# Two feed-forward layers that take over the buffers of the mixing stage before them

## The chip, the cores and the metric

The kernel runs as one launch on one core of a Trainium2 chip. A core has five engines that work from their own instruction queues: TensorE (PE, matrix products and transposes), VectorE (DVE), ScalarE (ACT), GpSimd (POOL) and SyncE (SP, which here issues nearly all transfers), and 16 DMA engines. The metric is the device time of one execution in microseconds (us). The kernel before takes 2841.91 us, the median of 3 runs that lie between 2841.21 and 2844.3 us.

## What is computed

Two transformer blocks, one behind the other, on a sequence of 1024 rows of 1024 float32 values. Each block mixes the rows (several kinds of attention, a convolution, a pooling), brings the mixed values back with a matrix `w_out`, and then runs a feed-forward network of 2816 channels. Cut to what surrounds the change:

```python
# first block
mix = concatenate([att, conv, pool], axis=-1)          # 1024 x 1024
x = x + mix @ w_out
h2 = rms_norm(x, norm2_g)
up = causal_depthwise_conv(h2 @ w_up, ffn_dw_w)        # 2 x 2816 columns
gate, val = split(up, 2)
x = x + (silu(gate) * val) @ w_down

# second block
merged = g_a * (y_a @ w_branch_a) + g_b * (y_b @ w_branch_b)
x = x + rmsnorm(merged @ w_out, post_mix_w)
h = rmsnorm(x, pre_ffn_w)
f = (silu(h @ w_gate) * (h @ w_up)) @ w_down
x = x + rmsnorm(f, post_ffn_w)
```

## The kernel before

**Numbers as pairs.** Every matrix operand is split into a rounded high part (a cast on ACT) and the rest (raw minus high, by DVE or POOL), and each product is three matmuls, high x high, low x high, high x low. A wide matmul has 512 columns. The tiles of a pair end in `h` and `l` (`T1h`, `T1l`), or are both called `w`.

**Stages, in the order of time.** `mix1` (attention, convolution, pooling) to about 420 us; `out1`, the first out projection, to 519.66; the first feed-forward layer's way up (`ffn_up`) to about 985 and its way down (`ffn_down`) to about 1200; `mix2` to about 1950 and `merge2` to about 2048; `out2`, the second out projection, to 2145; the second way up to 2610, the way down to the end. The program is written as a sequence of calls; a list scheduler puts each engine's instructions into one fixed order when the kernel is built, and on the chip each engine works that order off and waits on semaphores.

**The way up.** The 1024 rows and the inner dimension are halved, and per channel group of 128 seven products replace eight (a Strassen-like scheme). The seven right-hand operands `T1` to `T7` are normed rows, or sums of row blocks (L765 to L768 in `pre_row`), transposed through PE into a PSUM tile `tr` (L744) and split into high (ACT, L747) and low (DVE, L748) by `put`. `T1` and `T2` need rows 0 to 3 alone and are put as those rows come out of the out projection; the other five need rows 4 to 7, and their twenty puts follow the opening of the way up's own pools in the order `LATE = (6, 5, 7, 4, 3)`. The left-hand operands are 128 columns of the weights and sums of their quarters, split by ACT (L800) and, in turn, by POOL and DVE (`lo_of`, L787). A product goes into PSUM tiles `x`, `y` or `z`, which ACT copies (L843 snap).

**Pools.** `mixing` (L106) holds three pools for a mix and its out projection: `hT` (transposed rows, high and low, two halves), `w` (weights) and `ps` (PSUM, all eight banks). They close when the out projection is done; then `ffn` opens `fw` (weights), `fT` (T3 to T7) and a PSUM pool `fps`. A tile of a new pool can be written when the last readers and writers of the space below it are done.

**out1** (L690): row i takes two halves of 24 matmuls into `mm`, DVE adds each to the row in place (L706), then `done` stores the row to DRAM (`x1D`, L755), norms it in place (L186 to L188: square on ACT, mean and root on POOL, product on DVE) and puts it. **out2** (L1297) computes halves of eight rows (`first`, `second`) with half the weights each; per row two squares on ACT (L1318), POOL's sum and root, two products on DVE (L1323), the add (L1325), the store to `x3D` (L1326) and the norm. Rows come back from DRAM by eight loads on SP's queue (L1302), and its last three weight loads stand behind them.

The lines of a weight pair, which the prediction follows on ACT and POOL:

```python
# before, ffn_up
def split(raw, w):
    hi, lo = (fw.tile([P, 1024], F32R, tag="w", ...)[:, :w] for _ in range(2))
    nc.scalar.copy(out=hi, in_=raw)      # L800
    self.lo_of(lo, raw, hi)              # L787: POOL and DVE in turn
```

Of the kernel before, what the change touches and what calls it, by code (L numbers as in the profile page):

```python
# [41 lines left out]
LATE = (6, 5, 7, 4, 3)  # L42
# [39 lines left out]
class Net:  # L82
# [607 lines left out]
    def out1(self, rows, pp, done):  # L690
# [27 lines left out]
        gB, jk = (self.wpool.tile([P, D], F32, tag="wr", name=self.n("wr"), bufs=2) for _ in range(2))  # L718
        nc.sync.dma_start(out=gB, in_=I["norm2_g"][0].partition_broadcast(P))
# [13 lines left out]
    def early_T(self, name):  # L733

        keep, sums = ExitStack(), ExitStack()
        pool = keep.enter_context(self.pool(name, 1, side="right"))
        T = {i: tuple(pool.tile([P, 4, 512], F32R, tag=f"T{i}{x}", name=self.n(f"T{i}{x}")) for x in "hl") for i in (1, 2)}
        return keep, sums, sums.enter_context(self.pool(name + "s", 3, side="right")), T
# [11 lines left out]
    def pre_row(self, i, rows, keep, gB, jk, T, pool, ps):  # L750
# [3 lines left out]
        if keep is not None:  # L754
            nc.sync.dma_start(out=keep[i * P:(i + 1) * P, :], in_=x)  # L755
        self.norm_rows(x, x, jk, gB)
# [12 lines left out]
        self.sums[j] = {6: t2, 5: b11, 7: k0, 4: b21, 3: k1}  # L769

    def ffn(self, R, T, close_sums, close_T, Wg, cg, Wu, cu, Wd, conv, keep, done):

        gD = self.dram.tile([NF // 2, 7, P, 512], F32, tag=f"gD{int(conv)}", name=self.n("gD"))
        with self.pool("fw") as fw, self.pool("fT") as fT, self.pool("fps", 2, PSUM) as ps:
            self.ffn_up(T, fT, fw, R, ps, Wg, cg, Wu, cu, conv, gD, close_sums)
# [13 lines left out]
    def ffn_up(self, T, fT, fw, R, ps, Wg, cg, Wu, cu, conv, gD, close_sums):  # L789
        nc = self.nc  # L790
        chans, raws, pts = {}, {}, {}
# [4 lines left out]
        snaps = {1: t1, 2: t2, 3: t3}  # L796

        def split(raw, w):
            hi, lo = (fw.tile([P, 1024], F32R, tag="w", name=self.n("w"), bufs=8)[:, :w] for _ in range(2))
            nc.scalar.copy(out=hi, in_=raw)  # L800
            self.lo_of(lo, raw, hi)
            return [(hi[:, o:o + 512], lo[:, o:o + 512]) for o in range(0, w, 512)]

        def weights_a(c, queue=nc.sync):

            r = [fw.tile([P, 2, 512], F32, tag="wr", name=self.n("wr"), bufs=3) for _ in range(2)]
            for t, W, col in ((r[0], Wg, cg + c * P), (r[1], Wu, cu + c * P)):
                queue.dma_start(out=t.rearrange("p h (k m) -> p (h k) m", k=4),
                                in_=W[:, col:col + P].rearrange("(k p) m -> p k m", p=P))
            A = chans[c] = {}  # L810
            A[1], A[2] = split(r[0].rearrange("p h x -> p (h x)"), 1024)
            raws[c] = r

        def weights_b(c):

            r = raws.pop(c)
            A = chans[c]
            a11, a12, a21, a22 = r[0][:, 0], r[0][:, 1], r[1][:, 0], r[1][:, 1]
            u, v = (fw.tile([P, 2, 512], F32, tag="ws", name=self.n("ws"), bufs=2) for _ in range(2))
            nc.vector.tensor_tensor(out=u[:, 0], in0=a21, in1=a22, op=ALU.add)  # L820
            nc.vector.tensor_tensor(out=u[:, 1], in0=u[:, 0], in1=a11, op=ALU.subtract)
            A[5], A[6] = split(u.rearrange("p h x -> p (h x)"), 1024)
            nc.vector.tensor_tensor(out=v[:, 0], in0=a11, in1=a21, op=ALU.subtract)
            nc.vector.tensor_tensor(out=v[:, 1], in0=a12, in1=u[:, 1], op=ALU.subtract)
            A[7], A[3] = split(v.rearrange("p h x -> p (h x)"), 1024)
            A[4], = split(a22, 512)

# [11 lines left out]
        def begin(c):  # L839
            pts[c] = {n: ps.tile([P, 512], F32, tag=n, name=self.n(n)) for n in ("y", "x", "z")}  # L840

        def snap(c, j):
            nc.scalar.copy(out=snaps[j], in_=pts[c]["x"])  # L843
# [20 lines left out]
        def p3(c):  # L864
            product(c, 3, "y", False)
            add(c, G[:, 514:], "y", t2)
# [29 lines left out]
        for c in (0, 1):  # L896
            weights_a(c, nc.scalar)
        for i in (3, 4, 6, 7, 5):
            T[i] = tuple(fT.tile([P, 4, 512], F32R, tag=f"T{i}{x}", name=self.n(f"T{i}{x}")) for x in "hl")
# [546 lines left out]
```

## Time and profile before

| | |
|---|---|
| median of 3 runs (lowest, highest) | 2841.91 us (2841.21, 2844.3) |
| profiled execution, its own time | 2845.55 us |
| its span, first to last instruction | 2843.8 us |
| mean granted clock of TensorE over the span | 0.980 |
| PE busy | 2687.9 us (95%), 13686 matmuls |
| DVE busy | 1798.9 us (63%) |
| ACT busy | 1200.4 us (42%) |
| POOL busy | 891.6 us (31%) |

The busy share of PE is a mean over stages in which it never stops and stages in which it waits. Two things make PE late: idle time, and stretches in which its granted clock is at the lower of its two levels (1.2 instead of 2.4 GHz), where a matmul takes up to twice as long though PE counts as busy. So a stretch is read by three numbers together: busy time, number of matmuls, granted clock.

### The profile page before, as it was taken

The page shows a single profiled execution, that of the slowest core. Times are in us where ns is not written, and L with a number is a line of the kernel's source. Part 1 is how long each engine was busy: PE and PEld are TensorE (multiplying, and loading weights), DVE is VectorE, ACT ScalarE, POOL GpSimd, SP SyncE. Part 2 cuts the span into 40 slices and gives each one's busy share as a digit, 9 for nine tenths or more (in the row PEclk, how much of TensorE's full clock was granted, in tenths as well). Part 3 has the DMA queues.
Part 4 walks back from the last instruction along what each step waited for, and adds up shares of the span by engine and source line. Part 5 has one row for each costly group of instructions (what it writes and reads, how often), then busy time and mean ns, then how long its engine had stood idle before and what let it go on. Part 6 is the DMA issues. An engine that isn't in the chain of part 4 may idle for free.

```text
span 2843.8 us, 37039 instructions
## 1 busy us (share of the span) xinstructions
PE 2687.9 (95%) x13686; PEld 2258.3 (79%) x13686; DVE 1798.9 (63%) x2748; ACT 1200.4 (42%) x1879; POOL 891.6 (31%) x626
## 2 busy tenths in 40 slices
PE   8999889899999999999999999998997999999997
PEld 7799767678888778788888978887776788887786
DVE  4697574668878799736766443443427555555977
ACT  4344562344544543425545344444323333334333
POOL 3256322123333134611112254422423111211345
PEclk9999999999999999999999999999998999999999
DMA  5445342223332563265554495415412233335722
GB/s 182 122 124 146 115 158 97 82 78 100 107 111 97 207 244 122 93 194 139 155 162 128 126 209 140 133 62 180 157 77 78 82 102 106 111 101 191 260 89 93
DMA packets 317678, 374.01 MB, mean 132 GB/s; under 512 B 42613, under 2 KB 215089, under 8 KB 316985
## 3 DMA queue, kind: packets, MB, share of 16 engines
q1 hardware_dynamic: 309176, 367.45, 41.9%
q10 hardware_dynamic: 8320, 4.19, 0.5%
q8 instruction: 108, 1.77, 0.3%
q14 instruction: 74, 0.60, 0.1%
HBM read 256.49 MB, written 115.08 MB: 131 GB/s over the span
## 4 chain that ended last, share of the span: by engine, by line
PE 69%; DVE 10%; DMA 10%; issue 4%; POOL 3%; ACT 2%; SPq 1%; DVEq 0%; POOLq 0%; ACTq 0%
PE x L118 21%; PE mm L118 20%; PE y L118 11%; PE sc L118 5%; PE z L118 4%; PE pv L118 4%; DVE ac L550 2%; PE tr L359 2%; DVE x L1000 1%; DMA x<-in_w_down_dram 1%; PE tr L1105 1%; DMA x<-gD 1%; DMA mixD<-pvt 1%; DMA wr<-in_w_out_dram 1%; DVE r L1010 1%
## 5 line engine op out<-in xcount | busy, mean ns | idle before, releaser
L139 POOL TENSOR_TENSOR wl<-wr,wh 128x1024 fp32r<-128x1024 f32 x71 | 179.8, 2536 | 359.2 <-ACT wh L138 300.6
L787 POOL TENSOR_TENSOR hl<-x,hl 128x1024 fp32r<-128x1024 f32 x63 | 172.3, 2750 | 278.7 <-ACT hl L1031 197.9
L1031 ACT CAST hl<-x 128x1024 fp32r<-128x1024 f32 x154 | 153.2, 1050 | 221.9 <-PE x L118 123.5
L317 ACT ACTIVATE t<-t,mx 128x640 f32<-128x640 f32 (+3 forms) x192 | 172.9, 901 | 164.6 <-DVE mx L313 156.9
L118 PE MATMUL x<-hl,hl 128*128 128x512 f32 x704 | 214.1, 391 | 3.6 <-DVE hl L787 3.6
L787 POOL TENSOR_TENSOR w<-ws,w 128x1024 fp32r<-128x1024 f32 x44 | 135.4, 3078 | 250.7 <-ACT w L800 250.7
L787 POOL TENSOR_TENSOR w<-wr,w 128x1024 fp32r<-128x1024 f32 (+1 forms) x44 | 85.7, 1947 | 397.7 <-ACT w L800 397.7
L118 PE MATMUL mm<-hA,wh 128*128 128x512 f32 x608 | 197.6, 399 | 4.7 <-ACT gs L1231 4.7
L118 PE MATMUL mm<-hB,wh 128*128 128x512 f32 x608 | 196.7, 397 | 1.0 <-ACT gs L1231 1.0
L365 DVE TENSOR_TENSOR pl<-tr,ph 128x512 fp32r<-128x512 f32 (+2 forms) x160 | 100.5, 634 | 120.0 <-DMA yD<-pvt 42.6
L334 POOL TENSOR_SCALAR t<-t,rs 128x640 f32<-128x640 f32 (+7 forms) x128 | 107.4, 846 | 201.9 <-DVE rs L333 159.8
L877 DVE SCALAR_TENSOR_TENSOR r<-r,fdw,r 128x1024 f32<-128x1024 f32 x88 | 122.2, 1406 | 72.2 <-ACT r L875 72.1
L118 PE MATMUL y<-hl,hl 128*128 128x512 f32 x528 | 161.0, 390 | 5.7 <-DVE hl L787 5.7
L118 PE MATMUL mm<-wh,hB 128*128 128x256 f32 (+1 forms) x752 | 162.2, 305 | 3.0 <-ACT hB L180 3.0
L800 ACT CAST w<-wr 128x1024 fp32r<-128x1024 f32 (+1 forms) x88 | 73.6, 838 | 216.2 <-PE x L118 126.0
L118 PEld LDWEIGHTS x<-hl,hl 128*128 128x128 f32 x704 | 132.8, 189 | 32.3 <-DVE hl L787 4.8
L118 PE MATMUL mm<-wh,hA 128*128 128x256 f32 (+1 forms) x704 | 150.6, 301 | 6.3 <-ACT hA L180 2.1
L787 DVE TENSOR_TENSOR hl<-x,hl 128x1024 fp32r<-128x1024 f32 x91 | 140.7, 1553 | 8.7 <-ACT hl L1031 8.4
L118 PE MATMUL x<-hl 128*128 128x512 f32 x352 | 134.2, 393 | 4.9 <-DVE r L1010 4.7
L118 PEld LDWEIGHTS mm<-hA,wh 128*128 128x128 f32 x608 | 115.5, 192 | 29.2 <-ACT gs L1231 5.3
L843 ACT COPY r<-x 128x512 f32<-128x512 f32 x132 | 76.7, 581 | 145.4 <-PE x L118 87.1
L364 ACT CAST ph<-tr 128x512 fp32r<-128x512 f32 (+2 forms) x160 | 85.2, 542 | 123.7 <-PE tr L359 85.9
(350 smaller groups left out, 7720.5 us busy)
## 6 DMA issues: line engine op xcount, KB each, us to landing
gD<-r SPq DMA_DIRECT2D x154, 256.0 KB
x<-gD SPq DMA_DIRECT2D x154, 256.0 KB
wr<-in_w_up_dram SPq DMA_DIRECT2D x60, 512.0 KB
wr<-in_w_in_dram SPq DMA_DIRECT2D x50, 512.0 KB
x<-in_w_down_dram SPq DMA_DIRECT2D x88, 256.0 KB
wr<-in_w_gate_dram SPq DMA_DIRECT2D x20, 512.0 KB
wr<-in_w_out_dram SPq DMA_DIRECT2D x16, 512.0 KB
QS<-q2D SPq DMA_DIRECT2D x32, 256.0 KB
```

Source lines behind the costliest of these rows:

```text
L118: self.nc.tensor.matmul(out, lhsT, rhs, start=start, stop=stop, **kw)
L139: g = (lo_engine or nc.gpsimd).tensor_tensor(out=lo, in0=raw[:, :n], in1=hi.bitcast(F32), op=ALU.subtract)
L317: nc.scalar.activation(out=t[:, :nb * P], in_=t[:, :nb * P], func=AF.Exp, scale=-1.0, bias=m, accum_out=s)
L334: nc.gpsimd.tensor_scalar(out=t[:, :nb * P], in0=t[:, :nb * P], scalar1=r, scalar2=1.0, op0=ALU.mult, op1=ALU.mult)
L359: nc.tensor.transpose(tr[:, o * P:(o + 1) * P], ts[qb][:, c:c + P], self.ident)
L364: nc.scalar.copy(out=ph[:, :w], in_=tr[:, :w])
L365: nc.vector.tensor_tensor(out=pl[:, :w], in0=tr[:, :w], in1=ph[:, :w].bitcast(F32), op=ALU.subtract)
L787: return eng.tensor_tensor(out=lo, in0=raw, in1=hi.bitcast(F32), op=ALU.subtract)
L800: nc.scalar.copy(out=hi, in_=raw)
L843: nc.scalar.copy(out=snaps[j], in_=pts[c]["x"])
L877: nc.vector.scalar_tensor_tensor(out=t, in0=src[:, 2 - s:2 - s + S], scalar=self.fdw[:, 2 - s, cc:cc + 1], in1=t, op0=ALU.mult, op1=ALU.add)
L1031: nc.scalar.copy(out=hi, in_=raw)
```

## The change

The number of matmuls stays the same. The pools `hT` and `ps` of the mix now stay open through the way up, and close behind it (`close_mixing`). The way up's PSUM tiles take the mix's tags (`y` in `sc`, `x` in `mm`, `z` in `pv` or `sc`). T6 and T5 lie in the first halves of `hT` (`hA0`, `hB0`), T7 and T4 in the second, and only T3 in the pool `fT`. The puts of T6 and T5 move into the loop over rows 4 to 7, so 12 puts stay late. The first weight tile of the way up is loaded during the out projection and split there, by ACT and DVE (`w_early`), and the first pairs of channels 0 and 1 behind it are split by DVE instead of POOL. `out1` adds into a tile `o` (two buffers) and stores and norms from there. `out2` takes rows in turn: four halves first, then per row both halves, into one tile `o` (one buffer), with four of its eight weight pairs loaded by `pair_in` and split by DVE; the row loads stand ahead of `merge2`'s last weights in SP's queue.

```diff
-LATE = (6, 5, 7, 4, 3)
+LATE = (7, 4, 3)
...
-        with self.pool("hT", 2) as self.hpool, self.pool("w", 3) as self.wpool, self.pool("ps", 2, PSUM) as self.ps_mix:
+        stack = ExitStack()
+        self.hpool = stack.enter_context(self.pool("hT", 1))
+        self.ps_mix = stack.enter_context(self.pool("ps", 2, PSUM))
+        self.close_mixing = stack.close
+        with self.pool("w", 3) as self.wpool:
             yield
...
+    def T_in(self, t, h):
+        tile_ = self.h_tile(t, h)
+        return tile_[:, :4, :], tile_[:, 4:, :]
...
# out1
-        for i in range(NB):
-            part(i, 0, w0)
-            part(i, 1, w1[6:] if i < 4 else w1)
-            done(i, gB, jk)
+        with self.pool("pe") as pe:
+            gB = self.bcast_row(I["norm2_g"][0], pe)
+            self.w_early(pe.tile([P, D], F32, tag="o", name=self.n("o"), bufs=2))
+            for i in range(NB):
+                o = pe.tile([P, D], F32, tag="o", name=self.n("o"), bufs=2)
+                part(i, 0, w0, o)
+                part(i, 1, w1[6:] if i < 4 else w1, o)
+                done(i, gB, o)
...
# pre_row
+        if i == 4:
+            T[6], T[5] = self.T_in("hA", 0), self.T_in("hB", 0)
...
-        self.sums[j] = {6: t2, 5: b11, 7: k0, 4: b21, 3: k1}
+        self.put(T, 6, j, t2, ps)
+        self.put(T, 5, j, b11, ps)
+        self.sums[j] = {7: k0, 4: b21, 3: k1}
...
+    def w_early(self, raw):
+        raw = self.w_load(0, 0, raw.rearrange("p (h x) -> p h x", h=2))
+        self.w_split(0, (1, 2), raw.rearrange("p h x -> p (h x)"), self.nc.vector)
...
# ffn_up
-            pts[c] = {n: ps.tile([P, 512], F32, tag=n, name=self.n(n)) for n in ("y", "x", "z")}
+            pts[c] = {n: ps.tile([P, 512], F32, tag=t, name=self.n(n), bufs=b)
+                      for n, t, b in (("y", "sc", 3), ("x", "mm", 2), ("z", *(("sc", 3) if c % 2 else ("pv", 1))))}
...
         for c in (0, 1):
-            weights_a(c, nc.scalar)
+            weights_a(c, nc.vector)
...
# merge2
-            ws += self.pair(W, 6, 1, pool=po, th="wph", tl="wpl", bufs=1)
+            ws += self.pair_in(W, 6, 1, pp.tile([P, S], F32, tag="g0", name=self.n("g")), [(self.wpool, "wr", 2)] * 2)
...
+    def pair_in(self, W, k, dh, raw, hl):
+        nc = self.nc
+        nc.sync.dma_start(out=raw.rearrange("p (k m) -> p k m", k=2),
+                          in_=W[k * P:(k + 2) * P, dh * 512:(dh + 1) * 512].rearrange("(k p) m -> p k m", p=P))
+        hi, lo = (pool.tile([P, 1024], F32R, tag=tag, name=self.n(tag), bufs=bufs) for pool, tag, bufs in hl)
+        self.split(raw, hi, lo, nc.vector)
...
# out2
-            for i in range(4):
-                done(i, gB, None, True)
-            for i in range(4, NB):
-                o = second(i, w1)
-                done(i, gB, o, True)
+            half = [first(i) for i in range(4)]
+            for i in range(NB):
+                pts = (self.proj(i, mT, w0), half[i] if i < 4 else first(i))
+                o = pq.tile([P, D], F32, tag="o", name=self.n("o"))
...
+                nc.vector.tensor_tensor(out=o, in0=o, in1=rows[i][:, :D], op=ALU.add)
+                nc.sync.dma_start(out=yD[i * P:(i + 1) * P, :], in_=o)
+                done(i, gB, o)
```

PE's order where the first out projection ends, before: `mm` is row 7's last half, `tr` the transposes of T6, `x` and `z` the first products of the way up.

```order
L118 MATMUL mm_5454<-cB_5061,hB_4253 128x512
L118 MATMUL mm_5454<-KH_5060,hB_4254 128x512
L744 MATMUL tr_5533<-ident,t_1135_5347 128x128 [waits PE_49]
L744 MATMUL tr_5533<-ident,t_1135_5347 128x128 x3
L744 MATMUL tr_5540<-ident,t_1141_5394 128x128 x4
L118 MATMUL x_5548<-T1h_4805,w_5511 128x512 [waits Activation_49]
L118 MATMUL x_5548<-T1l_4806,w_5511 128x512
L118 MATMUL z_5549<-T2h_4807,w_5511 128x512
```

The same place after the change: the products of T1 and T2 with the early weights come ahead of and between the transposes of rows 6 and 7.

```order
L123 MATMUL x_5600<-T1l_4812,w_5163 128x512
L123 MATMUL x_5600<-T1h_4811,w_5164 128x512
L759 MATMUL tr_5497<-ident,t_1162_5492 128x128 [waits DVE_49,PE_49]
L759 MATMUL tr_5497<-ident,t_1162_5492 128x128 x3
L759 MATMUL tr_5504<-ident,r_1047_4796 128x128 [waits PE_49]
L759 MATMUL tr_5504<-ident,r_1047_4796 128x128 x3
L759 MATMUL tr_5559<-ident,t_1171_5554 128x128 [waits DVE_49,PE_49]
L759 MATMUL tr_5559<-ident,t_1171_5554 128x128 x3
L759 MATMUL tr_5566<-ident,r_1048_4797 128x128 [waits PE_49]
L759 MATMUL tr_5566<-ident,r_1048_4797 128x128 x3
L123 MATMUL x_5634<-T1h_4811,w_5591 128x512 [waits Activation_49]
L123 MATMUL x_5634<-T1l_4812,w_5591 128x512
```

What moved: before, `x` of channel 0 stands behind all of row 7 and waits for ACT's cast; after, twelve of its matmuls stand in front of `tr_5497`, and `z` of channel 0 (not shown) among the products of rows 5 to 7.

SP's queue at the second out projection before: `r` are the eight rows from DRAM, `wr` a weight pair, `gB` a gain.

```order
L1302 DMA r_3890_18997<-x2D 128x1024
L1302 DMA r_3891_18998<-x2D 128x1024
L163 DMA gB_19010<-in_post_mix_w_dram 128x1024
L163 DMA gB_19012<-in_pre_ffn_w_dram 128x1024
L135 DMA wr_19023<-in_w_out_dram 128x2x512
L135 DMA wr_19029<-in_w_out_dram 128x2x512
L135 DMA wr_19035<-in_w_out_dram 128x2x512
L1326 DMA x3D<-r_3884_18991 128x1024
```

After, the row loads stand further ahead, the first of them 44 rows before this piece; `g<-gD` are `merge2`'s gates, and the last weights go into `g` and `o`.

```order
L140 DMA wr_18973<-in_w_out_dram 128x2x512
L1306 DMA g_18833<-gD 128x1024
L1306 DMA g_18830<-gD 128x1024
L140 DMA wr_18979<-in_w_out_dram 128x2x512
L1306 DMA g_18908<-gD 128x1024
L1306 DMA g_18905<-gD 128x1024
L140 DMA wr_18985<-in_w_out_dram 128x2x512
L1333 DMA g_18991<-in_w_out_dram 128x2x512
L1333 DMA o_19031<-in_w_out_dram 128x2x512
L1333 DMA o_19037<-in_w_out_dram 128x2x512
L168 DMA gB_19063<-in_post_mix_w_dram 128x1024
```

What moved: the weights of `w_out_2` no longer follow the row loads in the queue.

ACT's order in the rows of the second out projection after the change, with what each instruction waits for: `o` is the one tile of a row, `sc` and `mm` its two halves.

```order
L1376 ACTIVATE o_19198,ms_3924_19200<-sc_19073 128x512 [waits DVE_49,PE_49]
L1376 ACTIVATE o_19198,ms_3923_19199<-mm_19173 128x512 [waits PE_49]
L198 ACTIVATE r_3888_19001,ms_19212<-o_19198 128x1024 [waits DVE_49]
L1376 ACTIVATE o_19258,ms_3935_19260<-sc_19098 128x512 [waits DMAHW1_49,DVE_49]
L1376 ACTIVATE o_19258,ms_3934_19259<-mm_19233 128x512 [waits PE_49]
L762 CAST T1h_19018<-tr_19219 128x4x128 [waits PE_49]
L762 CAST T2h_19020<-tr_19226 128x4x128 [waits PE_49]
L198 ACTIVATE r_3889_19002,ms_19272<-o_19258 128x1024 [waits DVE_49]
```

The same place before: the squares wait for PE alone.

```order
L1318 ACTIVATE o_19141,ms_3911_19142<-sc_19041 128x512 [waits PE_49]
L1318 ACTIVATE o_19212,ms_3921_19213<-sc_19066 128x512 [waits PE_49]
L1318 ACTIVATE o_19258,ms_3930_19259<-sc_19091 128x512 [waits PE_49]
L138 CAST woh_19025<-wr_19023 128x1024 [waits DMAHW4_49]
L138 CAST woh_19031<-wr_19029 128x1024 [waits DMAHW5_49]
L138 CAST woh_19037<-wr_19035 128x1024 [waits DMAHW6_49]
```

What is added is the wait of the first square of each row from the second on for a transfer (the store to `x3D` out of `o`) and for DVE (the norm's product, which reads `o`).

## Rows read from the trace of the kernel before

**Rows 1.** Windows: us, busy (count) of PE PEld DVE ACT POOL, clock, DMA

```profile
340.00:385.00 45.00, 35.25 (x206) 30.42 (x205) 31.09 (x95) 26.02 (x50) 15.59 (x22) 0.85 0.28 74
385.00:445.00 60.00, 51.67 (x274) 40.32 (x273) 37.72 (x81) 36.20 (x68) 17.97 (x14) 0.97 0.54 185
519.66:579.84 60.18, 48.15 (x217) 37.58 (x216) 39.53 (x52) 23.63 (x38) 13.30 (x7) 0.89 0.21 60
579.84:950.00 370.16, 370.16 (x1615) 301.72 (x1614) 293.46 (x306) 180.14 (x213) 118.24 (x38) 1.00 0.31 98
2048.55:2120.40 71.85, 64.79 (x267) 51.80 (x266) 18.27 (x18) 17.58 (x35) 20.50 (x26) 0.93 0.33 125
2120.40:2205.00 84.60, 68.13 (x311) 54.34 (x310) 58.05 (x76) 31.80 (x59) 24.48 (x24) 0.88 0.22 69
```

**Rows 2.** The same view, transposes of the puts (L744) alone

```profile
519.66:579.84 60.18, 12.11 (x80) 9.82 (x79) 0.89 0.21 60
...
2120.40:2205.00 84.60, 17.03 (x103) 13.32 (x101) 0.88 0.22 69
```

**Rows 3.** Waits of PE in 519.66 to 579.84: total us, times, longest

```profile
PE x L118 <- ACT w L800: 3.7, 1, 3.7
```

**Rows 4.** Timeline of PE in 519 to 540: start, us, instruction, idle before

```profile
524.89 0.63 PE L118 MATMUL x<-T1l,w 128*128 128x512 f32 x1
525.32 0.63 PE L118 MATMUL z<-T2h,w 128*128 128x512 f32 x1
...
537.55 0.60 PE L744 MATMUL tr<-ident,t 128*128 128x128 f32 x4
537.91 0.48 PE L118 MATMUL z<-T2h,w 128*128 128x512 f32 x1
```

**Rows 5.** Waits of PE in 2048.55 to 2120.4

```profile
PE mm L118 <- ACT woh L138: 3.6, 1, 3.6
```

**Rows 6.** Waits of PE in 2120.4 to 2205

```profile
PE tr L744 <- DVE t L766: 5.3, 2, 3.4
```

**Rows 7.** Timeline of SP in 2047 to 2085

```profile
2050.84 3.80 SPq L1302 DMA_DIRECT2D r<-x2D  x8
...
2057.64 15.42 SPq L135 DMA_DIRECT2D wr<-in_w_out_dram  x3
```

**Rows 8.** Timeline of DVE in 515 to 530

```profile
525.32 3.25 DVE L787 TENSOR_TENSOR w<-wr,w 128x1024 fp32r<-128x1024 f32 x1
```

**Rows 9.** Timeline of POOL in 515 to 545

```profile
524.93 2.57 POOL L787 TENSOR_TENSOR w<-wr,w 128x1024 fp32r<-128x1024 f32 x1
```

**Rows 10.** Groups of DVE in 2085 to 2165: busy, mean ns, idle before

```profile
L188 DVE SCALAR_TENSOR_TENSOR r<-r,rr,gB 128x1024 f32<-128x1024 f32 x8 | 12.4, 1544 | 11.5 <-DMA x3D<-r 11.0 <-POOL rr L158 0.4
L1325 DVE TENSOR_TENSOR r<-o,r 128x1024 f32<-128x1024 f32 x8 | 9.8, 1221 | 0.1
L1323 DVE SCALAR_TENSOR_TENSOR o<-mm,rr,gB 128x512 f32<-128x512 f32 x8 | 5.9, 742 | 0.0
...
L765 DVE TENSOR_TENSOR r<-r,r 128x512 f32<-128x512 f32 x3 | 2.1, 684 | 0.0
...
L787 DVE TENSOR_TENSOR w<-wr,w 128x1024 fp32r<-128x1024 f32 x1 | 1.2, 1224 | 0.2 <-ACT w L800 0.2
```

**Rows 11.** Groups of instructions of ACT in 2085 to 2165

```profile
L186 ACT ACTIVATE o<-r 128x1024 f32<-128x1024 f32 x8 | 8.5, 1062 | 15.6 <-DVE r L1325 15.6
L1318 ACT ACTIVATE o<-mm 128x512 f32<-128x512 f32 x7 | 4.2, 595 | 12.6 <-PE mm L118 12.6
...
L1318 ACT ACTIVATION_READ_ACCUMULATOR o<-mm 128x1 f32 x7 | 1.4, 194 | 0.0
```

**Rows 12.** Groups of instructions of POOL in 2085 to 2165

```profile
L158 POOL TENSOR_TENSOR rr<-rv,mhalf 128x1 f32<-128x1 f32 x16 | 9.7, 613 | 1.1
...
L156 POOL TENSOR_SCALAR rv<-ms 128x1 f32<-128x1 f32 x16 | 4.7, 297 | 25.8 <-ACT o L186 25.0
L1319 POOL TENSOR_TENSOR ms<-ms,ms 128x1 f32<-128x1 f32 x8 | 3.0, 380 | 29.6 <-ACT o L1318 29.6
```

More of the change, by code (lines that the diff above doesn't have):

```diff
@@ L735, in early_T @@
         keep, sums = ExitStack(), ExitStack()
+        self.early_hl = [keep.enter_context(self.pool(f"{name}w{i}", 1, side="right")) for i in range(2)]
         pool = keep.enter_context(self.pool(name, 1, side="right"))
         T = {i: tuple(pool.tile([P, 4, 512], F32R, tag=f"T{i}{x}", name=self.n(f"T{i}{x}")) for x in "hl") for i in (1, 2)}
-        return keep, sums, sums.enter_context(self.pool(name + "s", 3, side="right")), T
+        return keep, sums, sums.enter_context(self.pool(name + "s", 2, side="right")), T
     def put(self, T, i, col, src, ps):
@@ L795, in ffn_up @@
         gp = [R[5][:, :S], R[6][:, :S]]
[L796 to L812, printed above, removed]
@@ L814, in weights_b @@
-        def weights_b(c):
-            r = raws.pop(c)
-            A = chans[c]
-            a11, a12, a21, a22 = r[0][:, 0], r[0][:, 1], r[1][:, 0], r[1][:, 1]
[L819 to L826, printed above, removed]
+        snaps = {1: t1, 2: t2, 3: t3, (0, 2): R[2][:, :512], (NF - 1, 2): s1}
@@ L1295, in proj, with out2 @@
         return pt
-    def out2(self, mT, w1, xD, yD, rows, early, done):
+    def out2(self, mT, w1, xD, yD, rows, done):
         nc, I, ps = self.nc, self.I, self.ps_mix
         W = I["w_out_2"][0]
-        for i in range(NB):
-            nc.sync.dma_start(out=rows[i][:, :D], in_=xD[i * P:(i + 1) * P, :])
-        with self.pool("pq", 1) as pq:
+        with self.pool("p5", 4) as pp, self.pool("pq", 1) as pq:
+            w0 = []
+            for k in (0, 2, 4, 6):
+                raw = pq.tile([P, D], F32, tag="o" if k % 4 else "gf", name=self.n("o"))
+                w0 += self.pair_in(W, k, 0, raw, [(pp, "woh", 4), (pp, "wol", 4)])
+            for i in range(NB):
+                nc.sync.dma_start(out=rows[i][:, :D], in_=xD[i * P:(i + 1) * P, :])
@@ L1326, in second @@
-                nc.sync.dma_start(out=yD[i * P:(i + 1) * P, :], in_=x)
-                return o
-            with self.pool("p5", 1) as pp:
-                w0 = []
-                for k in (0, 2, 4, 6):
-                    w0 += self.pair(W, k, 0, pool=pp, th="woh", tl="wol", bufs=4)
-                for i in range(3):
-                    first(i, 1, w1)
-                for i in range(4):
-                    o = second(i, w0)
-                    done(i, gB, o, False)
-                    if i == 0:
-                        first(3, 1, w1)
-                for i in range(4, NB):
-                    first(i, 0, w0)
@@ L1364, in build, with early @@
     e = {}
-    def early(name):
-        e["keep"], e["sums"], e["pool"], e["T"] = net.early_T(name)
+    def early(*args):
+        e["keep"], e["sums"], e["pool"], e["T"] = net.early_T(*args)
     with net.mixing():
```

180 lines of the change are left out of this document (103 added, 77 removed).

## Prediction

> **What bounds the kernel now.** I read the page first: TensorE is busy for 95% of the span, and the number of matmuls is the same after the change, so only the time in which TensorE waits or runs at the lower clock can change. The share is a mean, so the second view was the table of windows, cut where the stages change [rows 1]. The reader is to see two kinds of stage there. On the first way up (579.84 to 950) TensorE is busy for all of 370.16 us, at a clock of 1.00, with 1615 matmuls, which makes 0.229 us for one. In the two hand-overs around 520 and around 2050 to 2205 it is not, and its clock is 0.88 to 0.93 of full speed.
>
> What a stretch loses is its length less its instructions at full speed: 0.229 us for a matmul, and 0.36 us for four transposes of a put (537.55 to 537.91) [rows 4].
> - A, 519.66 to 579.84, out1 to the way up: 217 instructions, 80 of them transposes [rows 1, 2]. 137 x 0.229 + 80 x 0.09 = 38.6 of 60.2 us: 21.6 lost.
> - B0, 2048.55 to 2120.4, merge to out2: 267 x 0.229 = 61.1 of 71.9 us: 10.8 lost.
> - B, 2120.4 to 2205, out2 to the second way up: 311, 103 of them transposes. 208 x 0.229 + 103 x 0.09 = 56.9 of 84.6 us: 27.7 lost.
> - C, 385 to 445, the end of attention: 60 less 51.67 is 8.3 idle; a clock of 0.97 over the busy time adds some 1.6. 10 lost. In 340 to 385, D, 9.75 are idle and a clock of 0.85 over 35.25 busy us costs about 5: 15 lost.
>
> That is 70 us in A, B0, B and C, and 85 with D. The third view, the waits, says who is late. In A it is ACT's cast of the first weights for 3.7 us [rows 3]; behind this wait matmuls start 0.43 us apart (524.89 to 525.32), half speed [rows 4]. In B0 it is the cast of out2's weights [rows 5], whose transfers SP issued from 2057.64 on, behind eight loads of rows issued from 2050.84 [rows 7]. In B it is DVE's sums for the late operands, 5.3 us in two waits [rows 6].
>
> **A: the first way up.** Removed: the wait for a new pool's space (early weights lie in tiles of their own), 8 of 20 late puts, and POOL's first split. After the change TensorE reaches row 7's last matmul at a time X and has 12 matmuls of the first product behind it (2.7 us) and two blocks of transposes. Then it needs row 7's first sum. The way there: DVE's add 0.7, ACT's square with its sum 1.25, POOL's mean and root 0.9, DVE's product 1.5, and three or four DVE instructions of 0.68, which is 7 to 8 [rows 10 to 12]; X+7.9 against X+3.4: about 4.5 us idle. Such an idle time is followed by half speed in A [rows 3, 4], so add 3 us. Of A's 21.6, 3.7 are the cast's and about 6.6 half speed (a clock of 0.89 over 60.2 us); the other 11 lie between the twenty late puts. Twelve stay, behind more products; I keep 3 us. Left: 0.5 + 4.5 + 3 + 3 = 11 of 21.6, a gain of 10.6; I take 10. The bounds are 3 (all late puts wait as before and half speed lasts twice as long) and 17 (row 7's wait is covered by the other products).
>
> **The norm no longer waits for the store.** In out2 DVE waited 11.0 us in four waits for `x3D`, 2.8 each [rows 10], because the norm wrote over the row that was being stored. Now it reads `o`. This is off TensorE's path in the first rows, since TensorE has products to do, and is part of A's and B's end only for row 7; it is in the chains above and below.
>
> **B0: out2's weights.** The row loads go ahead, so the weights no longer stand behind them. One pair still goes through POOL (2.57 us [rows 9]) and is needed some 19 matmuls, 4.3 us, behind the merge's last product; it is ready at about 4.5. The four pairs of the other half are split by DVE at 1.22 each [rows 10] and are needed some 14 us later, against about 12 by which the last is ready. So nearly all of the 10.8 goes: I take 10, with 5 and 11 as bounds, the lower if the loads into `o` and `gf` (one tile each, four loads) come one behind the other at the pace of the three in the rows, 15.4 us with the queue's waits [rows 7].
>
> When POOL splits at the same time, DVE's 1.22 us becomes 3.25 (525.32) beside POOL's 2.57 (524.93) [rows 8 to 10]. The Trainium skill says why: in the GPSIMD Engine Reference, section 1, Specifications, GpSimd's SBUF interfaces are shared with VectorE, with contention where a VectorE instruction has two SBUF inputs. The split is such an instruction, and the trace agrees. By that rule moving a split to DVE is no clean gain while POOL still splits: one of the four would be 2 us later, the last at 14, and B0 would give 8 instead of 10.
>
> **B: out2 in turn.** Per row of out2 there is now one chain, since `o` is one tile: two squares with their sums (0.6 + 0.19 each) 1.6, POOL's sum, mean and root 1.3 [rows 11, 12], two products 1.5, add 1.2, then the norm (square 1.25, mean and root 0.9, product 1.5) 3.7, while the store of `o` takes 2.8 [rows 10 to 12]. Together 9.3 us per row. TensorE's work for a row is 24 matmuls and 8 transposes in rows 0 to 3 (6.2 us, their other halves are done ahead) and twice the matmuls in rows 4 to 7 (11.7 us), 71.6 in all. The chain starts 5.5 us in and its last square may start at 5.5 + 7 x 9.3 = 70.6: just hidden. With two `mm` tiles the third to fifth row wait a little, up to 3.7 us. Behind row 7 come the first two channels' four products, 48 matmuls or 11 us, against a chain of about 9 + 4; some 2 us idle, and twelve late puts at 3 to 4 us. Left: about 9.5 of 27.7, a gain of 18. The bounds are 8 (chain at 10.5 us a row, and half speed behind the wait) and 24.
>
> **C and D: attention's end.** The order shows half of out1's 384 matmuls among attention's last products, before about 40 of them; loads of `w_out` and of the mixed rows go earlier in SP's queue. TensorE's 8.3 idle us of C can be filled. I take 8 of 10, and nothing in D, where the waits are for the softmax of heads that stay. Bounds 0 and 18.
>
> **Costs at nothing.** More splits fall to DVE on the ways up (half a us per channel); DVE is busy for 293 of 370 us there [rows 1], so this hides; without that cover it were 10 us per way up. The PSUM tags give each product the same two buffers as before. The ways down start from other tiles: between -2 and +2 us.
>
> **Sum.** 10 + 10 + 18 + 8 = 46 us. Against the profiled execution (2845.55 us, 1.75 more than its span) this makes 2799.5; the median of the runs is 3.6 lower, so 2796 us.
>
> **The rivals.**
> 1. Only the order of out2 counts (B0 and B), and A's wait for weights is replaced by the wait for row 7's sum at half speed, as the 4.5 us idle make likely; attention's end stays bound by its softmax. For it: in A DVE is busy 39.5 of 60 us, the most of any engine but TensorE [rows 1]. Then 10 + 14 + 3 = 27: 2815 us. Chance 0.2.
> 2. The free matmuls of out1 also fill D (half of its 15 us), and A and B lose half of what I left them: 46 + 7 + 10 = 63: 2779 us. Against it: early products need the mixed rows' loads, which come behind attention's own stores. Chance 0.16.
> 3. Slower: the single `o` makes the chain of out2, not TensorE, the bound. The place is ACT's first square of a row, which waits for the store to `x3D`; every us above 9.3 in the chain costs about 7 us over seven rows, so from 9.3 + 46/7 = 15.9 us a row on the kernel is slower than before. At 17 us it would be 2850. For it: POOL stretches DVE's instructions by up to 2.7 times [rows 8, 10], and the puts' casts queue between. Against it: POOL has nothing but small sums left there. Chance 0.05.
> 4. The change does not do what it says: the early weights' raw tile or the transposes of row 7 hold the products, and the new order loses elsewhere what it gains; within 5.7 us of before. Chance 0.06.
>
> **How the numbers follow.** The forecast has the rest, 0.53, with 2785 to 2808 as its own range. For 8 in 10 the range reaches over rival 2 at 2779 and its lower bounds, and over rival 1 at 2815 with half of its upper side: 2770 to 2824. A measurement can tell 0.2%, 5.7 us, from no change. Faster: 0.53 + 0.2 + 0.16 = 0.89; rivals 3 and 4 split the rest, 0.06 same and 0.05 slower.
>
> **What would show it.** In the new profile: TensorE's wait for the first `w` cast is gone, and the longest wait at the first way up is a transpose of T6 for DVE's sum, 3 to 6 us, with half speed behind it; no wait for `woh`; TensorE busy through out2's rows 4 to 7 with squares that wait for the store less than TensorE takes; 12 late puts. Wrong would be idle times of more than 2 us per row in out2, or a first stretch of attention (0 to 340) or a way up that has changed in length by more than 3 us.

## The result

The changed kernel takes 2809.98 us, the median of 4 runs (2808.77 to 2813.51), against 2841.56 us of the kernel before in the same rounds: 0.9888 of it, with a 95% interval of 0.9876 to 0.9901, or 31.6 us less. The forecast was 2796 us, 46 less, with a range of 2770 to 2824. A second measurement beside three of the experiments gave 2809.9 us (0.9890, 0.9876 to 0.9905). Where the forecast and the result part is read from stages, because one number hides terms that missed on either side.

The profiled execution has a span of 2807.0 us and a granted clock of 0.984; it is one of the faster ones, and that of before was one of the slower, so the two spans differ by 36.8 us where the medians differ by 31.6. Cut by TensorE's own marks (its last out1 matmul, the first product of a way down, and so on), the lengths of the stages are:

| stage, us | before | after | difference |
|---|---|---|---|
| start to the last matmul of out1 | 519.8 | 517.0 | -2.8 |
| to the first product of the way down (A) | 458.2 | 443.7 | -14.5 |
| first way down | 225.2 | 225.4 | +0.2 |
| mix2, to the last of its attention | 720.2 | 719.3 | -0.9 |
| merge2 and out2, to its last product (B0) | 221.8 | 216.9 | -4.9 |
| to the first product of the second way down (B) | 465.2 | 449.3 | -15.9 |
| second way down, to its last product | 216.3 | 218.4 | +2.1 |

Some work changes its stage. 28 of A's instructions (12 products of T2 and 16 transposes, 4.2 us at the prediction's rates) now stand ahead of out1's last matmul, and 16 of B's transposes (1.4 us) ahead of out2's.

The windows of the kernel after, at the stretches of [rows 1]: length, then busy time and instructions of PE, PEld, DVE, ACT and POOL, then granted clock, DMA share and GB/s.

```profile
385.00:465.00 80.00, 78.05 (x413) 63.78 (x412) 39.26 (x88) 39.88 (x72) 20.98 (x16) 0.98 0.40 140
516.99:580.00 63.01, 52.80 (x250) 42.72 (x250) 41.86 (x54) 29.65 (x43) 10.88 (x7) 0.96 0.24 71
580.00:950.00 370.00, 370.00 (x1613) 303.50 (x1612) 299.12 (x303) 176.92 (x211) 71.79 (x38) 1.00 0.33 107
1905.34:1952.00 46.66, 37.69 (x144) 29.12 (x145) 12.94 (x20) 21.66 (x31) 5.78 (x3) 0.89 0.76 273
2030.00:2100.00 70.00, 69.31 (x319) 57.00 (x318) 33.24 (x35) 21.55 (x43) 11.48 (x26) 1.00 0.22 80
2117.53:2190.00 72.47, 63.16 (x283) 49.34 (x283) 46.42 (x62) 30.17 (x48) 15.86 (x12) 0.93 0.27 84
```

With idle time plus the length times one less the clock as a stretch's loss, out2's start (2030 to 2100) now loses 0.7 us where [rows 1] had 7.1 idle and a clock of 0.93, 12.1 in all. By the same sum A falls from 18.7 [rows 1] to 12.7, and B from 26.6 [rows 1] to 14.4. The way up itself is the same up to 950 us (370 of 370). But the merge's start, 1905 to 1952, is a stretch that the prediction did not speak of; here is the same piece of the kernel before:

```profile
1923.44:1970.00 46.56, 39.51 (x163) 31.47 (x164) 15.43 (x23) 23.40 (x34) 9.99 (x6) 0.96 0.65 207
```

It lost 8.9 us there and loses 14.1 now. The waits of TensorE name the reason (total us, times, longest; the first line is the only wait of the kernel before, the others are those after), and SP's timeline its place:

```profile
PE mm L118 <- ACT gs L1231: 7.1, 4, 3.5
...
PE mm L123 <- ACT gs L1276: 3.5, 1, 3.5
PE mm L123 <- ACT wh L143: 2.5, 1, 2.5
PE mm L123 <- ACT yh L132: 1.6, 1, 1.6
PE mm L123 <- POOL wl L144: 1.1, 1, 1.1
```

```profile
1912.51 9.20 SPq L1361 DMA_DIRECT2D r<-x2D  x7
...
1924.58 0.38 SPq L140 DMA_DIRECT2D wr<-in_w_branch_a_dram  x1
```

The row loads that no longer stand ahead of out2's weights [rows 7] now stand ahead of the merge's: seven of them hold the queue for 9.2 us, and `wr` of the merge is issued at 1924.58.

At the two hand-overs the waits of TensorE are now these, first A (516.99 to 580), then B (2117.53 to 2190):

```profile
PE tr L759 <- DVE t L781: 4.3, 1, 4.3
PE x L123 <- ACT r L892: 4.3, 1, 4.3
PE y L123 <- DVE r L885: 1.4, 1, 1.4
```

```profile
PE x L123 <- ACT w L815: 2.7, 1, 2.7
PE tr L759 <- DVE t L781: 2.6, 1, 2.6
PE y L123 <- DVE r L885: 2.3, 2, 1.4
```

The casts of channel 0 [rows 3] and of `woh` [rows 5] are gone. In their place stands row 7's sum (`t`), in A also ACT's copy of a product out of PSUM (`r`, the snap), and in B the first weights of channel 1 (`w`).

One more place has changed, of which the prediction does not speak: the end of each way up. Here are the last 28.05 us of the first one, before and after, and TensorE's waits in them:

```profile
950.00:978.05 28.05, 24.51 (x99) 18.92 (x98) 18.17 (x19) 11.54 (x15) 2.81 (x1) 0.94 0.68 233
932.65:960.70 28.05, 26.61 (x117) 21.26 (x115) 20.85 (x23) 13.25 (x17) 3.61 (x2) 1.00 0.53 178
```

```profile
PE x L118 <- ACT r L843: 3.4, 2, 2.7
PE x L123 <- ACT r L892: 0.7, 1, 0.7
```

In the same time TensorE does 18 matmuls more, 4.1 us of work; at the second way up's end it is 14 more in 28.4 us, 3.2 us. Before, the copy of the last channel's product starts at 966.41, behind a sum of DVE that reads the copy before it (964.64); after, it goes into a buffer of its own (`snaps` in the changed code) and starts at 946.04, where nothing waits for it. No run takes this edit alone.

### The profile page after: what moved, and what is told of

It reads as the page before. It is cut to its first block, busy times and chain, and to the rows that moved or that the text cites. A ratio compares the mean times of both kernels' runs of the same rounds, so it can differ in the third digit from the quotient of the medians.

```text
span 2807.0 us, 37030 instructions
## 1 busy us (share of the span) xinstructions
PE 2672.8 (95%) x13686; PEld 2250.9 (80%) x13686; DVE 1812.3 (65%) x2756; ACT 1202.7 (43%) x1881; POOL 822.8 (29%) x618
## 4 chain that ended last, share of the span: by engine, by line
PE 74%; DVE 9%; DMA 9%; issue 3%; POOL 2%; ACT 2%; SPq 1%; DVEq 0%; POOLq 0%; ACTq 0%
PE mm L123 24%; PE x L123 21%; PE y L123 12%; PE sc L123 5%; PE z L123 4%; PE pv L123 4%; DMA x<-in_w_down_dram 2%; DVE ac L562 2%; PE tr L371 2%; DMA x<-gD 1%; DMA mixD<-pvt 1%; DVE x L1045 1%; DMA wr<-yD 1%; PE tr L1150 1%; DVE pl L377 1%
## 5 line engine op out<-in xcount | busy, mean ns | idle before, releaser
L123 PE MATMUL x<-hA,w 128*128 128x512 f32 x1056 | 257.3, 395 | 4.5 <-ACT r L892 4.3
L123 PE MATMUL mm<-hA,wh 128*128 128x512 f32 x608 | 243.6, 401 | 3.5 <-ACT gs L1276 3.5
L123 PE MATMUL mm<-hA,wl 128*128 128x512 f32 x608 | 241.4, 397 | 0.0
L123 PEld LDWEIGHTS x<-hA,w 128*128 128x128 f32 x1056 | 200.0, 190 | 48.0 <-ACT r L892 5.5
L123 PE MATMUL mm<-wh,hA 128*128 128x256 f32 (+1 forms) x704 | 210.6, 299 | 3.9 <-ACT hA L192 3.3
L123 PE MATMUL mm<-wh,hB 128*128 128x256 f32 (+1 forms) x704 | 210.4, 299 | 1.2 <-DVE hB L193 1.2
L123 PE MATMUL mm<-wl,hA 128*128 128x256 f32 (+1 forms) x704 | 209.2, 297 | 0.9 <-DVE wl L144 0.9
L840 POOL TENSOR_TENSOR w<-wr,w 128x512 fp32r<-128x512 f32 x42 | 54.8, 1304 | 459.0 <-ACT w L815 459.0
L840 DVE TENSOR_TENSOR w<-wr,w 128x1024 fp32r<-128x1024 f32 (+1 forms) x42 | 52.0, 1238 | 178.3 <-ACT w L815 172.9
L815 ACT CAST w<-wr 128x512 fp32r<-128x512 f32 (+1 forms) x86 | 71.7, 833 | 207.1 <-PE x L123 115.5
```

Source lines behind the costliest of these rows:

```text
L123: self.nc.tensor.matmul(out, lhsT, rhs, start=start, stop=stop, **kw)
L815: self.nc.scalar.copy(out=hi, in_=raw)
L840: return eng.tensor_tensor(out=lo, in0=raw, in1=hi.bitcast(F32), op=ALU.subtract)
```

## The experiments

Each was timed in five rounds against the kernel before, in three groups (its medians there are 2841.61, 2839.43 and 2840.65 us). "The change" is the changed kernel at 2810 us. The interval of a ratio reaches some 3 to 4 us to either side, as much as many of the differences between two variants. So a difference is held against the stages: behind the first 520 us they agree within 0.4 us between two executions of the change, all but mix2 (3.2 us).

Two things in the traces bear on all of these runs. TensorE's order is the same in every kernel for its first 2168 instructions, to about 350 us. And its order in the second way down is one of two, chosen by the scheduler, though no edit touches that stage: the kernel before, T5 late (the first of the two), row 7's sum first, channel 1's weights first and both repairs take 215.5 to 216.3 us there, the change and all others 218.2 to 219.2. Up to 3 us of a difference can come from that alone.

**Four tags alone.**

```diff
 # before.py
-        parts = [[self.hpool.tile([P, 8, 512], F32R, tag=t, name=self.n(t)) for _ in range(2)] for t in ("hA", "hB")]
-        return [p[0] for p in parts], [p[1] for p in parts]
+        return [[self.hpool.tile([P, 8, 512], F32R, tag=f"{t}{h}", name=self.n(t)) for h in range(2)] for t in ("hA", "hB")]
```

> The kernel before with one edit: the transposed rows get four tags of one buffer each (hA0, hA1, hB0, hB1) instead of two tags of two. In the order of the instructions this alone brings half of out1's matmuls among attention's last products, as after the whole change. Theory (the gain of about 8 us from the start to out1's end comes from this order): 2833 to 2835 us against 2841.6, the last out1 matmul at 510 to 513 us instead of 519.8, and no change behind it. Rival (that gain needs the early weights or the add into a tile of its own): within 2 us of before. Second rival (the earlier loads only move attention's waits): slower by up to 3 us.

2837.53 us, 0.9991 (0.9980 to 1.0001): by the ratio a gain of 2.6 us, with an interval that includes no change. Its last out1 matmul ends at 514.6 us instead of 519.8. But that mark is at 517.0 and 524.3 us in two executions of the changed kernel, and 5.3 of these 7.4 us have arisen by TensorE's 2000th instruction, at 313 to 318 us, where all kernels still have the same order. From there to out1's last matmul the kernel before takes 206.5 us, the next run, which leaves this stage as it was, 207.2, and this one 199.8. So in its stage the order is worth about 6.7 us, near the 8 expected, and 2.7 of them are lost again in the second way down, which has the other order here (219.0 for 216.3).

**Rows behind the weights.**

```diff
 # before.py, out2: the eight loads moved behind the four weight pairs
+                for i in range(NB):
+                    d = nc.sync.dma_start(out=rows[i][:, :D], in_=xD[i * P:(i + 1) * P, :])
+                    self.tc.add_manual_dep(d.ins, self.last_w, NOSYNC, reason="rows behind")
...
```

> The kernel before with the eight loads of x2D rows put behind the last three loads of out2's weights in SP's queue. Theory (the 11 to 12 us lost at 2048 to 2120 are the weights that stand behind 4 MB of rows): 2830 to 2834 us, and the waits for the cast woh (3.6 us) and the split wol (1.2 us) gone. Rival (two raw tiles and POOL's splits of 2.4 us each set the pace): a gain under 3 us, the wait for woh replaced by one for wol. Rival on the other side: the first rows' adds now wait for x2D, and it is slower.

2835.14 us, 0.9980 (0.9970 to 0.9990), 5.7 to 6.5 us less. The stretch from the merge's start to out2's last matmul shrinks from 221.8 to 213.6. SP's timeline, to be held against [rows 7]:

```profile
2050.93 9.21 SPq L135 DMA_DIRECT2D wr<-in_w_out_dram  x3
2060.19 3.93 SPq L1332 DMA_DIRECT2D r<-x2D  x8
```

The waits for `woh` and `wol` are gone from 2045 to 2140, and the one for POOL's `wl` (2.2 us) stays. So the queue's order was the cause of most of B0. Moving the rows behind costs nothing at their use: no wait of DVE or TensorE in 2045 to 2140 is for them. In the time 2.9 us of the 8.2 are lost again in the second way down, which has the other order (219.2 for 216.3).

**No early weights.**

```diff
 # after.py, in out1 and in out2
-            self.w_early(pe.tile([P, D], F32, tag="o", name=self.n("o"), bufs=2))
...
-            self.w_early(pq.tile([P, D], F32, tag="o", name=self.n("o")))
```

> The changed kernel without the early load and split of the first weight tile: channel 0's first operands are split when the way up's pool is open. Theory (early weights cover row 7's chain): the wait for the cast comes back on both ways up, 3 to 4 us and as much half speed each: 2818 to 2825 us against 2810. Rival (TensorE then waits for row 7's first sum anyway, so products only change places): 2809 to 2812.

2809.53 us, 0.9894 (0.9880 to 0.9908): the same as the change. The rival holds. TensorE's waits in 510 to 580 of this run:

```profile
PE x L123 <- ACT r L891: 4.3, 1, 4.3
PE x L123 <- ACT w L814: 2.7, 1, 2.7
PE y L123 <- DVE r L884: 1.4, 1, 1.4
PE x L123 <- DVE w L818: 1.2, 1, 1.2
```

The wait for weights is back (2.7 and 1.2), and the wait for row 7's sum (4.3) is gone: the products that were done early now stand where TensorE waited for that sum, and cover it. In A one of the two is uncovered in either kernel; in B of this run both stand, 3.8 us for the sum in two waits and 1.3 for the cast. The copy (`r`, 4.3 us) stands in both kernels.

**T5 late.**

```diff
 # after.py, pre_row and ffn_up
-        self.put(T, 5, j, b11, ps)
-        self.sums[j] = {7: k0, 4: b21, 3: k1}
+        self.sums[j] = {5: b11, 7: k0, 4: b21, 3: k1}
...
         snap(0, 1)
+        puts(5)
         puts(7)
```

> The changed kernel with the four puts of T5 late again, behind the first four products of the way up, 16 late puts instead of 12. Theory (each late put costs TensorE some 0.6 us where no product is left to cover it): 2812 to 2816 us over both ways up. Rival (products and puts cover one another, and the row loop gets four puts lighter, so row 7's sum is ready sooner): 2806 to 2810.

2819.48 us, 0.9923 (0.9910 to 0.9937), 9.5 slower than the change. Here one put reads a source that the first snap has already written over: it waits for the snap, and a part of T5 comes from other numbers. So this run does not price the four puts alone; the next one takes this out:

```diff
-        snap(0, 1)
         puts(5)
+        snap(0, 1)
```

> As t5_late, with T5's four late puts ahead of the first snap (which writes over one of their sources) instead of behind it: 16 late puts against 12. Theory (late puts without cover cost about 2 us each on the two ways up together): 2814 to 2820 us, the first way up 5 to 8 us longer than after the whole change (443.7 us from out1's last matmul to the way down). Rival (what t5_late measured was its place behind the snap): 2809 to 2812.

2817.64 us, 0.9919 (0.9905 to 0.9934): 7.7 slower, over two ways up, as the theory has it. The first stretch from out1 to the way down is 450.2 us long against 443.7 (and 443.7 in the second execution of the change), the second 454.9 against 449.3. Among TensorE's waits in 517 to 585 there is a new one beside the old, for the low part of a put:

```profile
PE tr L759 <- DVE t L781: 4.8, 1, 4.8
PE x L123 <- ACT r L891: 4.3, 1, 4.3
PE tr L759 <- DVE hB L763: 2.1, 1, 2.1
```

Taking back four of the eight puts that were moved, with the order that the scheduler then makes, costs a quarter of the whole gain.

**Rows in the middle of the merge.**

```diff
 # after.py, out2
+                self.tc.add_manual_dep(d.ins, self.gate_dma[2 if i < 4 else 4], NOSYNC, reason="late rows")
...
```

> The changed kernel with the x2D row loads held back until merge2's third and fifth channel group in SP's queue, instead of issued at its start (1909 to 1922 us). Theory (4 MB of rows ahead of merge2's first weights cost 5 us at 1935 to 1947: waits for wh 2.5, wl 1.1, yh 1.6 and half speed): 2804 to 2806 us, these waits gone. Rival (the waits are the last attention output's way through DRAM, and only change their name): within 2 us of 2810. Rival on the other side (the loads now collide with gates and weights in the middle of the merge, which has no idle time now): slower by 2 to 5 us.

2806.46 us, 0.9877 (0.9864 to 0.9891), 3.4 less than the change beside it (2809.9). In the merge's start only one kind of wait is left:

```profile
PE mm L123 <- ACT gs L1276: 7.2, 2, 3.8
```

Those for `wh` and `wl` are gone, and the one for `gs` has doubled, to what it was in the kernel before (7.1 in four waits). Merge and out2 take 213.7 us, 3 less than in the change (216.9 and 216.6) and as long as in the run with the rows behind the weights (213.6). By idle time and clock the merge's start loses 10.5 us here, 14.1 in the change and 8.9 before. Whether the rows cost by their place in the queue or by their 4 MB on the way at the same time, no run separates.

**Row 7's sum first.**

```diff
 # after.py, ffn_up, for channels 0 and 1
+                    self.tc.add_manual_dep(d.ins, self.t2_ins, NOSYNC, reason="sum first")
...
```

> The changed kernel with the first sums of channels 0 and 1's weights held behind row 7's sum for T6 on DVE, on both ways up. Theory (TensorE's waits for that sum, 4.3 and 2.6 us, are partly DVE's weight sums in front of it): 1.8 us sooner on the first way up and 2 to 5 on the second, with less half speed: 2803 to 2807 us. Rival (the weights' sums are then late for the product of T6 by as much): within 2 us of 2810.

2805.89 us, 0.9874 (0.9859 to 0.9890), 4.0 less than the change beside it. The wait in A falls from 4.3 to 3.1 and that in B is gone. But waits for weights come in their place (0.7 in A; 3.4 where 2.7 stood, and 1.7 for POOL's split, in B), and the two hand-overs together are no shorter: A takes 445.6 us, B 1.6 less by the mark of its last matmul. 2.9 us of the gain lie in the second way down (215.5 for 218.4), which has the other order here: a wait of 1.8 us at 2632 is not there. The time agrees with the theory, its place mostly doesn't.

**Channel 1's weights first.**

```diff
 # after.py, ffn_up
+        for c, j in ((0, 1), (1, 0), (0, 0), (1, 1)):
+            self.w_load(c, j)
+        raws[0].reverse()
```

> The changed kernel with channel 1's first weights loaded ahead of the second load of channel 0's (order: 0's second tile, 1's first, 0's first, 1's second). Theory (TensorE's wait of 2.7 us for that cast at 2131 is the third of four transfers of 512 KB in a row): the wait falls to about 1.4 us: 2807 to 2809 us. Rival (the cast waits for ACT's squares of row 7 ahead of it, or channel 0's tile is now late by as much): no change, 2809 to 2811.

2816.01 us, 0.9911 (0.9897 to 0.9925): 6.1 slower, which neither side expected. The wait for the cast falls from 2.7 to 1.0 us, as said, but the scheduler orders other instructions anew. Merge and out2 become 4.5 us longer, A some 4 and B 2.4, and B waits for row 7's sum instead:

```profile
PE tr L759 <- DVE t L781: 7.5, 1, 7.5
PE tr L759 <- DVE hA L763: 1.7, 2, 1.0
```

It does not tell what the load alone is worth.

**Splits by POOL.**

```diff
 # after.py, ffn_up
-            weights_a(c, nc.vector)
+            weights_a(c)
...
-                weights_b(0, second=False, eng=nc.vector)
+                weights_b(0, second=False)
```

> The changed kernel with the first splits of channels 0 and 1 behind the early one given to POOL and DVE in turn again, as before the change. Theory (POOL's splits of 2.4 us stretch DVE's instructions beside them, among them row 7's chain): 2812 to 2816 us, with DVE's norm product or sums at 2 to 3.4 us again in both hand-overs. Rival (DVE is relieved of two splits of 1.2 us there, which pays for it): 2806 to 2810.

2814.35 us, 0.9907 (0.9892 to 0.9921), 4.4 slower. DVE's timeline at row 7:

```profile
525.29 2.83 DVE L781 TENSOR_TENSOR t<-r,r 128x512 f32<-128x512 f32 x1
```

Beside a split of 2.67 us on POOL from 524.90 on, the sum takes 2.83 us instead of 0.68, and TensorE waits 6.5 us for it instead of 4.3; A is 3.3 us longer, B 1.6. What [rows 8, 9] showed for a split happens here to a sum that reads two operands from SBUF, the one that TensorE waits for. It does not happen to the low parts of two puts, which read one of their operands from PSUM: they take 0.69 and 0.68 us (2137.20 and 2137.81) beside a split of 2.53 us on POOL from 2136.76 on.

**Both repairs, with and without early weights.** The edits of the rows in the middle of the merge and of the sum together, then also without `w_early`.

> The changed kernel with the x2D loads in the middle of the merge and row 7's sum ahead of the weights' sums, the two edits of x2d_mid_merge and sum_first. They act in different places, so the gains of 3.4 and 4.0 us should add: 2802 to 2804 us against 2810 of the change. Rival (the sum's gain was in part a shift of phase behind the merge): 2805 to 2807.

2799.10 us, 0.9851 (0.9836 to 0.9866), 10.9 less than the change and below both ranges. That this is more than the two gains of 7.4 added is not shown: the intervals are too wide for it. By the stages 3.3 us of it lie in merge and out2, 2.2 in B and 2.9 in the second way down, where the order is the other one: 8.4, of which 5.5 lie where the two edits act.

> As both_fixes, without the early load and split of the first weights. Theory (early weights and row 7's sum cover each other: with the sum earlier, TensorE's wait is the weights' alone): 2803 to 2808 us, 1 to 4 slower than both_fixes. Rival (worth nothing here as without the fixes): the same as both_fixes within 1 us.

2797.46 us, 0.9852 (0.9836 to 0.9869): the same, so the rival holds again. The two are the fastest kernels here; the windows of the first at the merge's start, out2's start and B:

```profile
1902.56:1950.00 47.44, 40.19 (x162) 32.60 (x163) 15.34 (x24) 23.86 (x34) 11.33 (x6) 0.93 0.66 206
2020.00:2090.00 70.00, 69.31 (x317) 56.96 (x316) 31.62 (x33) 21.97 (x42) 11.62 (x23) 1.00 0.26 90
2111.45:2184.00 72.55, 63.93 (x293) 50.50 (x293) 47.14 (x62) 29.68 (x48) 13.14 (x12) 0.95 0.27 84
```

## Why the prediction was right, and where its sum was off

The sign and the range held; the sum was 46 us where 31.6 came. By its terms:

**A, 10 us, came out at 10, in part by luck.** The stretch is 14.5 us shorter, of which 4.2 are the instructions that moved ahead of it: 10.3 are left. But by the prediction's own count the hand-over (516.99 to 580; 64 of its 250 instructions are transposes) still loses 14.7 us of 21.6, a gain of 6.9. The rest lies at the way up's end, for which the prediction has no term. The wait for row 7's sum was put at 4.5 us and is 4.3, by luck too: the terms of its path add up to 6.4 to 7.1 us and not to the 7.9 that the prediction went on with. What it did not see is in DVE's order and makes up for that: two weight sums and a low part stand between the first sum and the one that TensorE waits for, 1.8 us. DVE's timeline of the changed kernel:

```profile
521.71 0.68 DVE L780 TENSOR_TENSOR r<-r,r 128x512 f32<-128x512 f32 x1
522.31 0.68 DVE L864 TENSOR_TENSOR ws<-wr 128x512 f32<-128x512 f32 x1
522.91 0.68 DVE L763 TENSOR_TENSOR hB<-tr,hB 128x512 fp32r<-128x512 f32 x1
523.51 0.68 DVE L870 TENSOR_TENSOR ws<-wr,wr 128x512 f32<-128x512 f32 x1
524.11 0.68 DVE L781 TENSOR_TENSOR t<-r,r 128x512 f32<-128x512 f32 x1
```

The 3 us that were kept for late puts are not there (0.2 us of waits). In their place is a wait that was not seen, as long as the one for row 7: 4.3 us at 573.8 for ACT's copy of channel 1's `x`. In ACT's order this copy (L892) stands behind the gate of channel 0 (L928), with a table load and a wait for DVE in front of it. ACT's timeline of the changed kernel:

```profile
572.94 1.28 ACT L928 ACT_TABLE_LOAD   x1
575.62 1.06 ACT L928 ACTIVATE r<-r 128x1024 f32<-128x1024 f32 x1 [1.40 <-DVE r L926]
576.88 0.59 ACT L911 COPY r<-x 128x512 f32<-128x512 f32 x1 [0.19 <-DVE r L926]
577.42 0.59 ACT L892 COPY r<-x 128x512 f32<-128x512 f32 x1
```

Before, the same load (585.62) and gate came while TensorE had products of T5 to do, and it waited for nothing there. All variants of the change have this wait, 4.3 us long, and no run takes it away.

The removed wait for the early weights was named first among A's gains. It gave nothing (no early weights); the puts inside the row loop did (T5 late), and the splits that left POOL (splits by POOL). Rival 1 had this half: the wait for weights is replaced by that for the sum.

**B0, 10 us, was right at its place (11.4) and wrong in its balance.** The step that failed is "the row loads go ahead", priced at nothing: their new neighbours in SP's queue were not named. They cost the merge's start 5.2 us, and merge and out2 together gain 4.9, or 6.3 with the transposes that moved in. Some 3 us came back when the loads were moved on. The queue's order alone, in the kernel before, makes merge and out2 shorter (213.6) than the whole change does (216.9).

**B, 18 us, was too large.** By the prediction's count the hand-over (2117.53 to 2190; 72 of its 283 instructions are transposes) still loses 17.7 us of 27.7, where 9.5 were left to it: a gain of 10.0. The whole stage is 15.9 us shorter, 14.5 without the moved transposes, and 3.2 of these lie at its end. Two things were left out of the sum. The way up's raw weight tiles lie where row 7's products still read, so SP waits for out2's last product and issues their transfers from 2122.11 on, and channel 1's first is the third of them. ACT waits for it, and TensorE for ACT. SP's and ACT's timelines of the changed kernel:

```profile
2122.11 0.38 SPq L801 DMA_DIRECT2D wr<-in_w_gate_dram  x1
2122.55 1.26 SPq L801 DMA_DIRECT2D wr<-in_w_up_dram  x1
2123.90 1.11 SPq L801 DMA_DIRECT2D wr<-in_w_gate_dram  x1
```

```profile
2130.26 1.04 ACT L815 CAST w<-wr 128x1024 fp32r<-128x1024 f32 x1 [5.19 <-DMA wr<-in_w_gate_dram]
```

And half speed was not counted there, behind this wait and, for longer, behind that for row 7's sum (a clock of 0.93 over 72.47 us is 5.1 us); the sum had 2 us of idle time there and no more.

**Rival 3's chain is there, but not where it was put.** Rows follow one another by 9.96 us (first squares at 2113.84 and 2123.80), 9.3 was worked out; they wait for DVE's norm product, which reads `o`, and not for the store. TensorE waits for this chain once, 0.5 us. ACT's timeline of the changed kernel:

```profile
2113.84 0.60 ACT L1376 ACTIVATE o<-sc 128x512 f32<-128x512 f32 x1 [1.51 <-DVE r L200]
...
2123.80 0.60 ACT L1376 ACTIVATE o<-sc 128x512 f32<-128x512 f32 x1 [1.60 <-DVE r L200]
```

**C, 8 us, was sized nearly right.** The order did what was said (2 us idle of 80 in 385 to 465), though 340 to 388 lost 5 us more than 340 to 385 before. From TensorE's 2000th instruction to out1's last matmul the change takes 204.1 and 206.1 us in two executions, with 4.2 us more of work in it, against 206.5 and 207.2 without it: 4.6 to 7.3 us less, and 6.7 with the order alone (four tags).

**The bounds "between -2 and +2" for the ways down** were just passed in the second: +2.1, the price of the slower of its two orders.

**Taken together,** the hand-over of A gave 6.9 us, B0 6.3, that of B 10.0 and C some 6 or 7, which is 30 of the 46; the ways up's ends, without a term in the sum, gave 7.3, and the ways down took 2.3. That makes about 35, at the upper end of what the times allow (28 to 35); the rest is in the first 313 us and mix2, which differ between executions. Without those ends the time would have been some 7 us longer, still inside the range: the range held by its width, and that the miss is not larger is luck.

The prediction weighed POOL's splits against those on DVE in B0. There they did no harm: DVE's five splits take 1.2 us each (2040.94 to 2051). POOL's splits decide elsewhere, in DVE's chain at row 7. The Trainium skill (GPSIMD Engine Reference, section 1, Specifications) says that GpSimd shares its SBUF interfaces with VectorE, with contention for a VectorE instruction with two SBUF inputs. By that rule POOL's splits slow this chain, and the run with them agrees, 2.83 us for 0.68 and 4.4 us in the time.

## What to carry to other kernels

A transfer that is taken out of one stage's way is put in another's: name what it stands in front of at its new place, as for any instruction that moves. Where two chains end at the same hand-over (weights and a last row), removing one wait shows the other, so price the pair and not the first of them; here the gain came from the work that left the hand-over altogether. Read the order of the engine that the waiting one depends on: cheap instructions ahead of the one that is awaited are a wait. And read the far end of a stage too: a term can come out right because a gain there makes up for a miss at its start. When a scheduler sets the order, compare the orders of stages that no edit touches before a gain of 3 us is put down to the edit.

## What was not expected of the hardware

The granted clock fell behind shorter waits than the 3.70 us of [rows 3, 4] too. In B of the changed kernel TensorE waits 2.73 us, and a little later matmuls start 0.43 us apart (2133.75 and 2134.18, half speed). In the kernel before they do so behind 2.19 us (2054.18 and 2054.61). TensorE's timeline of the changed kernel:

```profile
2131.36 0.50 PE L123 MATMUL x<-T1h,w 128*128 128x512 f32 x1 [2.73 <-ACT w L815]
...
2133.75 0.63 PE L123 MATMUL x<-T1l,w 128*128 128x512 f32 x1
2134.18 1.05 PE L123 MATMUL x<-T1h,w 128*128 128x512 f32 x2
```

And the same program's first 520 us differ by 7.4 us between executions (517.0 and 524.3 us to out1's last matmul), while all later stages agree within 0.4 us but one (mix2, 3.2 us): a stage can be less steady than the whole.
